# The down projection of a hybrid encoder block: kept activation sums, one more unit by seven products, weight loads in order

## The chip, the cores and the metric

The kernel runs on one core of a Trainium2 chip. The metric is the device time of one execution in microseconds. The median of three runs of the kernel before is 1112.83 us (1112.75 to 1113.62).

## The reference

One layer of an encoder block over 256 tokens of width 2048, in float32. After a mixing sub-layer (which the change doesn't touch) come a gated feed-forward part and a gated embedding:

```
hn   = rmsnorm(h, ffn_norm_pre)
up   = hn @ w_ffn_up                                  # 2048 -> 2 x 5632
gate, val = split(up, 2)
gate = dwconv_centred(gate, ffn_conv_w, ffn_conv_b)   # three taps along the tokens
ff   = (gelu(gate) * val) @ w_ffn_down                # 5632 -> 2048, "down"
h    = h + rmsnorm(ff, ffn_norm_post)
gate = sigmoid(rmsnorm(h, ple_norm_pre) @ w_ple_gate) # 2048 -> 2048
h    = h + rmsnorm(gate * (p @ w_ple), ple_norm_post)
```

## The kernel before

**Products.** Every float32 operand is split in two float32r parts, a high one (a cast, on ScalarE, L153) and a low one (the rest, a subtraction on VectorE, L154), by `split`. A product is then three matmuls: high by high, high by low, low by high. Matmuls have 128 x 128 stationary activations and 512 columns of weight.

**Down.** The hidden activations (44 blocks of 128 rows by 256 tokens, in six pages named `hid`) are multiplied by `w_down` in two column halves of 1024 (`sublayer`, which calls `token_major` once a half; names with `dn0` and `dn1`). Within a half the 44 blocks are taken in 22 units of two, u = 0 to 21. A plain unit loads one raw page of weight (128 x 2048, 1 MB), splits it in two pieces of 1024 columns and issues 24 matmuls. A unit named in `fast` (`dn_fast`, 17 units in the first half, 15 in the second) goes to `seven_products` instead: it treats the unit as a 2 x 2 block product and computes it with seven block products, 21 matmuls, at the price of sums. It needs sums of weight blocks (`add_blocks`, four additions of 128 x 512), and sums of activation blocks (`hid_sums`). After the last such unit `combine` adds the parts together. PSUM has six main banks and two others.

**Where the sums come from.** The weight sums are made ahead of time, during the gate/value matmuls of the feed-forward part: `block_sums` gives three jobs, fetch (a load on SP's queue), add (VectorE) and store (to DRAM, on POOL's queue). The list `which` names these units, and job i is placed at piece 45*i//10 + 4 of the 176 pieces of that stage, its add and store three pieces later; the last two stay in their pages. Down then loads the sums (tile names ending in `t`) beside the raw weight's last 1536 columns (names ending in `r`); the four splits of a unit are named `a` (512 columns of raw weight), `b` (1024 of raw weight), `d` and `c` (1024 each of the sums). The activation sums of thirteen pairs (`dn_stored`) are made in the same stage, stored to DRAM, and loaded back on POOL's queue into one of three `mid` tiles (L1096, names `hd`). The pairs of units 4, 9, 12 and 15 are not stored: `hid_sums` computes them in Down with four small VectorE operations (L826 to L829), a cast (L830) and a subtraction (L831), in each half anew. Each unit also splits its two activation blocks (`hid_split`, L968 and L969, two `hs` tiles).

**Output of a half.** After each half four 128 x 512 pieces are scaled and multiplied by the norm's gain into two pages `mg` (L877), one for each group of 128 tokens, both taken at the start of `sublayer`. After both halves the residual `h` (L887) is formed and transposed for the gate matmul.

**Order.** The framework schedules each engine's instructions by priority, dependence and free buffers; program order is the priority. `in_order` fixes the order by hand in the gate/value stage only. `load` issues a DMA on SP's queue; unless it is called with `ahead`, it is tied behind the last load that was noted in `last["dma"]`. The raw weight and sums loads are called with `ahead`, so the scheduler may swap them with each other. SP's queue works strictly in the order that results, and a load whose buffer isn't free holds those behind it. There are 13 pages of 128 x 2048 (hidden rows, sums, outputs), three raw tiles, five high and five low split tiles.

**The gate's first tile.** `at={11: first}` makes the second half of Down load the first tile of `w_gate` into a page (`gtf`) and split it into two more before unit 11, so that the gate matmul after Down can start at once. At the end of the second half (`NF // 2`) the residual is loaded back (`hb`) and the embedding's weight is split.

Of the kernel before, what the change touches and what calls it, by code (L numbers as in the profile page):

```python
# [17 lines left out]
P = 128  # L18
# [35 lines left out]
def build(nc, a, out):  # L54
# [6 lines left out]
    with tile.TileContext(nc) as tc, \  # L61
# [95 lines left out]
        def raw(name, src=None):  # L157
            r = wp.tile([P, 2048], F32, tag="raw", bufs=3, name=name)
            if src is not None:
                last["dma"] = load(r, src, True)  # L160
            return r

        class Panel:
# [28 lines left out]
                                                       op0=ALU.mult, op1=ALU.subtract)))  # L192

        LOW_LAST = (0, 2), (1,)
        work = []

        chain = {}
# [62 lines left out]
            nc.gpsimd.dma_start(t, r)  # L260
            sums_["wo", c * 1024, k] = t, False

        def add_blocks(r):

            v = r.rearrange("p (b c) -> p b c", b=4)
            for i, j in ((1, 0), (0, 3), (3, 1), (2, 3)):
                nc.vector.tensor_add(v[:, i], v[:, i], v[:, j])  # L267

        def seven_products(name, stage, w, k0, c0, a_, acc, alt, start, stop):

            if (stage, c0, k0) in sums_:
                r = raw(f"{name}r")
                last["dma"] = load(r[:, 512:], w[c0 // 1024, k0 // 2][:, 512:], True)
                t, held = sums_[stage, c0, k0]
                if not held:
                    t = page(f"{name}t")
                    last["dma"] = load(t, sums_[stage, c0, k0][0], True)
            else:  # L280
                r = t = raw(f"{name}r", w[c0 // 1024, k0 // 2])
            b11 = split(f"{name}a", r[:, 512:1024], 512)
            b2 = split(f"{name}b", r[:, 1024:], 1024)
            if r is t:
                add_blocks(r)
            t42 = split(f"{name}d", t[:, 1024:], 1024)
            t31 = split(f"{name}c", t[:, :1024], 1024)

            for x, (wh, wl), c, o, own in (
                    ("a11", b11, 0, alt[0], True), ("a12", b2, 0, acc[0][0], False), ("a22", t42, 0, acc[1][0], False),  # L290
                    ("s4", b2, 512, acc[0][1], False), ("s2", t42, 512, alt[3], True), ("s1", t31, 512, alt[1], True),
                    ("s3", t31, 0, alt[2], True)):
                xh, xl = a_[x]
                for q, (xx, ww) in enumerate(((xh, wh), (xh, wl), (xl, wh))):
                    mm(o, xx, ww[:, c:c + 512], own and start and q == 0, own and stop and q == 2)
# [561 lines left out]

        def sublayer(name, w, ks, get, gain, h, vnext, panel=Panel, fast=((), ()), sums=None, at=(), row=None, then=()):

            mg = [page(f"{name}m{t}") for t in range(2)]  # L860
            sq = [[], []]
            for half in range(2):

                alt = main(f"{name}s{half}") if fast[half] and half == 0 else []
                acc = [main(f"{name}a{half}{t}") for t in range(2)]
                if fast[half]:
                    alt += main(f"{name}s{half}") if half else []
                token_major(f"{name}{half}", w, half * 1024, ks, get, acc, 1, fast[half], alt, sums, at if half else ())
                for t in range(2):
                    for n in range(2):  # L870
                        q = tiny(f"{name}q{t}{half}{n}", 1)
                        junk = sp.tile([P, 512], F32, tag="junk", bufs=1, name=f"{name}j{t}{half}{n}")
                        c = slice(half * 1024 + n * 512, half * 1024 + (n + 1) * 512)
                        b = acc[t][n]
                        if row:
                            nc.scalar.activation(junk, b, AF.Square, scale=row[t], accum_out=q)
                            nc.vector.scalar_tensor_tensor(mg[t][:, c], b, row[t], gain[:, c], op0=ALU.mult, op1=ALU.mult)  # L877
                        else:
                            nc.scalar.activation(junk, b, AF.Square, accum_out=q)
                            nc.vector.tensor_mul(mg[t][:, c], b, gain[:, c])  # L880
                        sq[t].append(q)
            r = [rms(f"{name}{t}", sq[t], 1.0 / D) for t in range(2)]
            pan = panel(f"{name}x")
            for c in range(4):
                s = slice(c * 512, (c + 1) * 512)
                for t in range(2):
                    nc.vector.scalar_tensor_tensor(h[t][:, s], mg[t][:, s], r[t], h[t][:, s],  # L887
                                                   op0=ALU.mult, op1=ALU.add)
# [50 lines left out]
        for t in range(2):  # L939
            h_kept.append(dp.tile([P, D], F32, tag=f"h{t}", bufs=1, name=f"h_kept{t}"))  # L940
        pl_kept = dp.tile([P, D], F32, tag="pl", bufs=1, name="pl_kept")

        dn_fast, gt_fast = ((2, 3, 4, 5, 7, 8, 9, 10, 11, 12, 13, 14, 15, 16, 17, 18, 19), (2, 3, 4, 5, 7, 8, 9, 11, 12, 13, 14, 15, 16, 18, 19)), ((4, 5, 6), (1, 2, 3))

        dn_stored = (2, 3, 5, 7, 8, 10, 11, 13, 14, 16, 17, 18, 19)
        gt_ks = list(range(NK)), [0, 1, 8, 9, 10, 11, 12, 13, 2, 3, 4, 5, 6, 7, 14, 15]
        which = [("dn", w_down, c * 1024, 2 * u) for c in range(2) for u in dn_fast[c]] + \
            [("gt", w_gate, c * 1024, gt_ks[c][2 * u]) for c in range(2) for u in gt_fast[c]]
        jobs_at = [[] for _ in range(NPIECES)]

# [133 lines left out]
        def hid_get(k):  # L1084
# [47 lines left out]
        pl = [page("plb")]  # L1132
# [161 lines left out]
```

## Time and profile before

| what | value |
|---|---|
| median of three runs | 1112.83 us |
| the profiled execution | 1112.05 us |
| its span, first to last instruction | 1110.3 us |
| granted TensorE clock, mean | 0.997 |
| down, first half | 784.61 to 883.65 us |
| down, second half | 883.65 to 1006.12 us |

The page gives busy times by engine over the span; the windows give the same by stage, with the number of instructions in brackets, the granted clock, the busy share of the 16 DMA engines and what they moved. The chain of waits lists, in order of time, the work that ended last at each moment: start, length, engine, tile. A timeline row gives start and duration of one instruction and, in square brackets, how long its engine was idle before it and what ended that. PE is TensorE's matmul stream, PEld its weight loads, DVE VectorE, ACT ScalarE, POOL GpSimd, SPq the DMA queue of SyncE. A matmul of 512 columns is shown with about 0.39 us though the next starts 0.23 us later, so its row doesn't give its price; the distance of starts does.

### The profile page before, as it was taken

To read this page: it belongs to the slowest core of one execution; us is meant where nothing else is said; L and a number is where in the kernel's file an instruction comes from. 1 tells how busy PE (TensorE), PEld (TensorE's weight loads), DVE (VectorE), ACT (ScalarE), POOL (GpSimd) and SP (SyncE) were. 2 spreads that over 40 slices of the span, in tenths; PEclk is the share of its full clock that TensorE was granted. 3 is DMA by queue.
4 is the path that set the end of the run, shared out by engine and by line. 5 is a ranking of instruction groups with operands and counts; after the bars stand their busy time and mean duration, and the time that the engine had idled before them with its cause. 6 is when DMAs were issued, how large, how long until landed. Compare 5 with 4: busy or idle time off the path is not lost.

```text
span 1110.3 us, 16102 instructions
## 1 busy us (share of the span) xinstructions
PE 1101.8 (99%) x5958; PEld 950.0 (86%) x5958; DVE 968.6 (87%) x1351; ACT 727.8 (66%) x1061; POOL 78.1 (7%) x144
## 2 busy tenths in 40 slices
PE   9999999999999999999999999999999999999997
PEld 9999988888888888888888888888888888888875
DVE  6589997898868998888888888988899999999996
ACT  7958763555775565655655646657579877877682
POOL 0200000100100000000000000000000000021001
PEclk9999999999999999999999999999999999999998
DMA  9984356555589999999999998999999799995772
GB/s 364 367 332 185 115 197 259 208 218 201 182 344 399 397 416 349 384 365 361 391 362 379 359 390 342 405 355 424 362 390 401 299 341 408 412 391 225 276 294 76
DMA packets 56671, 358.83 MB, mean 323 GB/s; under 512 B 6288, under 2 KB 7184, under 8 KB 20880
## 3 DMA queue, kind: packets, MB, share of 16 engines
q1 hardware_dynamic: 45216, 296.87, 67.9%
q0 software_dynamic: 10944, 60.30, 14.4%
q8 instruction: 47, 0.77, 0.3%
q10 hardware_dynamic: 432, 0.62, 0.2%
q14 instruction: 32, 0.26, 0.1%
HBM read 304.82 MB, written 52.95 MB: 322 GB/s over the span
## 4 chain that ended last, share of the span: by engine, by line
PE 93%; ACT 3%; DMA 2%; DVE 1%; issue 1%; POOL 0%; SPq 0%; POOLq 0%; ACTq 0%
PE ga L90 22%; PE va L90 22%; PE dna L90 12%; PE woa L90 7%; PE xbc L90 5%; PE gt L90 5%; PE z L90 4%; PE dns L90 4%; PE dn0s L90 2%; PE dn1s L90 2%; DMA dtur<-w_dtu 2%; PE ple L90 1%; PE gts L90 1%; DMA x<-x 1%; PE yd L90 1%
## 5 line engine op out<-in xcount | busy, mean ns | idle before, releaser
L90 PE MATMUL ga<-wox,ug_0h 128*128 128x512 f32 x352 | 125.5, 395 | 0.0
L90 PE MATMUL ga<-wox,ug_1h 128*128 128x512 f32 x352 | 125.1, 394 | 0.0
L90 PE MATMUL va<-wox,uv_1h 128*128 128x512 f32 x352 | 124.8, 393 | 0.0
L90 PE MATMUL va<-wox,uv_0h 128*128 128x512 f32 x352 | 124.8, 393 | 0.0
L90 PE MATMUL ga<-wox,ug_1l 128*128 128x256 f32 x352 | 99.1, 282 | 0.0
L90 PE MATMUL va<-wox,uv_1l 128*128 128x256 f32 x352 | 99.1, 281 | 0.0
L90 PE MATMUL va<-wox,uv_0l 128*128 128x256 f32 x352 | 99.1, 281 | 0.0
L90 PE MATMUL ga<-wox,ug_0l 128*128 128x256 f32 x352 | 99.0, 281 | 0.0
L267 DVE TENSOR_TENSOR dnb<-dnb 128x512 f32<-128x512 f32 x128 | 88.3, 690 | 3.1
L90 PEld LDWEIGHTS va<-wox,uv_1h 128*128 128x128 f32 x352 | 66.1, 188 | 15.0
L90 PEld LDWEIGHTS va<-wox,uv_0h 128*128 128x128 f32 x352 | 66.1, 188 | 15.0
L90 PEld LDWEIGHTS ga<-wox,ug_1h 128*128 128x128 f32 x352 | 66.1, 188 | 15.0
L90 PEld LDWEIGHTS ga<-wox,ug_0h 128*128 128x128 f32 x352 | 66.1, 188 | 14.8
L90 PEld LDWEIGHTS ga<-wox,ug_0l 128*128 128x128 f32 x352 | 66.2, 188 | 0.1
L90 PEld LDWEIGHTS ga<-wox,ug_1l 128*128 128x128 f32 x352 | 66.2, 188 | 0.0
L90 PEld LDWEIGHTS va<-wox,uv_1l 128*128 128x128 f32 x352 | 66.2, 188 | 0.0
L90 PEld LDWEIGHTS va<-wox,uv_0l 128*128 128x128 f32 x352 | 66.2, 188 | 0.0
L245 POOL DMA_DIRECT2D dns<-dnb x30 | 16.1, 535 | 320.4 <-DVE dnb L267 291.6
L968 ACT CAST hs<-hid 128x512 fp32r<-128x512 f32 x44 | 27.1, 619 | 17.2 <-PE dna L90 17.1
L830 ACT CAST he<-he 128x512 fp32r<-128x512 f32 x13 | 8.1, 621 | 41.1 <-DVE he L829 41.1
L969 DVE TENSOR_TENSOR hs<-hid,hs 128x512 fp32r<-128x512 f32 x44 | 29.9, 685 | 3.4 <-ACT hs L968 3.4
L90 PE MATMUL dna<-dn_0h,hs 128*128 128x512 f32 x96 | 31.2, 393 | 0.0
(2334 smaller groups left out, 3249.6 us busy)
## 6 DMA issues: line engine op xcount, KB each, us to landing
dnb<-w_down SPq DMA_DIRECT2D x32, 1024.0 KB, 10.0
dns<-dnb POOLq DMA_DIRECT2D x30, 1024.0 KB, 5.8
hd<-hsum POOLq DMA_DIRECT2D x24, 512.0 KB, 8.4
zr<-w_z SPq DMA_DIRECT2D x8, 1024.0 KB, 4.8
dtur<-w_dtu SPq DMA_DIRECT2D x14, 528.0 KB, 8.7
dn1r<-w_down SPq DMA_DIRECT2D x7, 1024.0 KB, 9.3
hsum<-he POOLq DMA_DIRECT2D x13, 512.0 KB, 8.5
wo0r<-w_out_ SPq DMA_DIRECT2D x6, 1024.0 KB, 4.8
```

Source lines behind the costliest of these rows:

```text
L90: last["pe"] = ins(nc.tensor.matmul(o, lhsT, rhs, start=start, stop=stop, skip_group_check=True))
L245: nc.gpsimd.dma_start(t, pg[0])
L267: nc.vector.tensor_add(v[:, i], v[:, i], v[:, j])
L830: nc.scalar.copy(o[:, :512], s[:, :512])
L968: nc.scalar.copy(t[:, :512], hid_part(k))
L969: nc.vector.tensor_sub(t[:, 512:], hid_part(k), t[:, :512].bitcast(F32))
```

## The change

- The activation sums of units 4, 9, 12 and 15 are computed once, in the first half, into two pages (two pairs to a page), and used again in the second half.
- Unit 10 of the second half goes by seven products too (16 units instead of 15).
- In the second half, units 4 and 10 (`dn_here`) don't use stored weight sums: they load the whole raw page and add the blocks on the spot, on VectorE, into a fresh page. Unit 4's fetch, add and store leave the gate/value stage, and the list `which` has 37 entries instead of 38.
- The loads of the second half (`IN_ORDER`, names that begin with `dn1`) are each tied behind the load before.
- The gate's first tile is loaded before unit 15 (`first_raw`) and split before unit 17 (`first`).
- The pages of the weighed output hold one column half each instead of one token group each, and are taken at the end of their half.

```diff
         def raw(name, src=None):
             r = wp.tile([P, 2048], F32, tag="raw", bufs=3, name=name)
             if src is not None:
-                last["dma"] = load(r, src, True)
+                last["dma"] = load(r, src, not name.startswith(IN_ORDER))
             return r
...
+        IN_ORDER = ('dn1',)
...
+        APART = ("dn",)
+
-        def add_blocks(r):
+        def add_blocks(r, t=None):
 
             v = r.rearrange("p (b c) -> p b c", b=4)
-            for i, j in ((1, 0), (0, 3), (3, 1), (2, 3)):
-                nc.vector.tensor_add(v[:, i], v[:, i], v[:, j])
+            s = v if t is None else t.rearrange("p (b c) -> p b c", b=4)
+            for i, a, b in ((1, v, 0), (0, v, 3), (3, s, 1), (2, s, 3)):
+                nc.vector.tensor_add(s[:, i], v[:, i], a[:, b])
...
             if (stage, c0, k0) in sums_:
                 r = raw(f"{name}r")
-                last["dma"] = load(r[:, 512:], w[c0 // 1024, k0 // 2][:, 512:], True)
+                last["dma"] = load(r[:, 512:], w[c0 // 1024, k0 // 2][:, 512:], not name.startswith(IN_ORDER))
                 t, held = sums_[stage, c0, k0]
                 if not held:
                     t = page(f"{name}t")
-                    last["dma"] = load(t, sums_[stage, c0, k0][0], True)
+                    last["dma"] = load(t, sums_[stage, c0, k0][0], not name.startswith(IN_ORDER))
             else:
                 r = t = raw(f"{name}r", w[c0 // 1024, k0 // 2])
+                if stage in APART:
+                    t = page(f"{name}t")
+                    add_blocks(r, t)
...
-            mg = [page(f"{name}m{t}") for t in range(2)]
+            mg = []
...
                 token_major(f"{name}{half}", w, half * 1024, ks, get, acc, 1, fast[half], alt, sums, at if half else ())
+                mg.append(page(f"{name}m{half}"))
...
-        dn_fast, gt_fast = ((2, 3, 4, 5, 7, 8, 9, 10, 11, 12, 13, 14, 15, 16, 17, 18, 19), (2, 3, 4, 5, 7, 8, 9, 11, 12, 13, 14, 15, 16, 18, 19)), ((4, 5, 6), (1, 2, 3))
-
+        dn_fast, gt_fast = ((2, 3, 4, 5, 7, 8, 9, 10, 11, 12, 13, 14, 15, 16, 17, 18, 19), (2,3,4,5,7,8,9,10,11,12,13,14,15,16,18,19)), ((4, 5, 6), (1, 2, 3))
+
+        dn_here = (), (4,10,)
...
-        which = [("dn", w_down, c * 1024, 2 * u) for c in range(2) for u in dn_fast[c]] + \
+        which = [("dn", w_down, c * 1024, 2 * u) for c in range(2) for u in dn_fast[c] if u not in dn_here[c]] + \
...
+        own, own_pages = {}, []
+
         def hid_sums(k):
 
             (h1, l1), (h2, l2) = get_hid(k), get_hid(k + 1)
-            o = mid(f"hd{k}", F32R)
             if k in kept:
+                o = mid(f"hd{k}", F32R)
                 nc.gpsimd.dma_start(o.bitcast(F32), kept[k])
                 d = sums_in(o)
             else:
-                d = hid_sums_of(k, sp.tile([P, 512], F32, tag="junk", bufs=1, name=f"hs{k}"), o)
+                if k not in own:
+                    n = len(own)
+                    if n % 2 == 0:
+                        own_pages.append(page(f"hd{k}", F32R))
+                    own[k] = hid_sums_of(k, sp.tile([P, 512], F32, tag="junk", bufs=1, name=f"hs{k}"),
+                                         own_pages[-1][:, n % 2 * 1024:(n % 2 + 1) * 1024])
+                d = own[k]
...
+        def first_raw():
+
+            cur["gtf"] = page("gtf")
+            last["dma"] = load(cur["gtf"], w_gate[0, 0])
+
         def first():
 
-            r, hi, lo = page("gtf"), page("gtfh", F32R), page("gtfl", F32R)
-            last["dma"] = load(r, w_gate[0, 0])
+            r, hi, lo = cur.pop("gtf"), page("gtfh", F32R), page("gtfl", F32R)
...
-                      fast=dn_fast, sums=hid_sums, at={11: first, NF // 2: lambda: (ple_parts(), back())}, row=rf, then={1: lambda: second(0), 2: lambda: second(1)})
+                      fast=dn_fast, sums=hid_sums, at={15: first_raw, 17: first, NF // 2: lambda: (ple_parts(), back())}, row=rf, then={1: lambda: second(0), 2: lambda: second(1)})
```

More of the change, by code (lines that the diff above doesn't have):

```diff
@@ L871, in sublayer @@
                         q = tiny(f"{name}q{t}{half}{n}", 1)
+                        m = mg[half][:, t * 1024 + n * 512:t * 1024 + (n + 1) * 512]
                         junk = sp.tile([P, 512], F32, tag="junk", bufs=1, name=f"{name}j{t}{half}{n}")
@@ L876, in sublayer @@
                             nc.scalar.activation(junk, b, AF.Square, scale=row[t], accum_out=q)
-                            nc.vector.scalar_tensor_tensor(mg[t][:, c], b, row[t], gain[:, c], op0=ALU.mult, op1=ALU.mult)
+                            nc.vector.scalar_tensor_tensor(m, b, row[t], gain[:, c], op0=ALU.mult, op1=ALU.mult)
                         else:
                             nc.scalar.activation(junk, b, AF.Square, accum_out=q)
-                            nc.vector.tensor_mul(mg[t][:, c], b, gain[:, c])
+                            nc.vector.tensor_mul(m, b, gain[:, c])
                         sq[t].append(q)
@@ L886, in sublayer @@
                 for t in range(2):
-                    nc.vector.scalar_tensor_tensor(h[t][:, s], mg[t][:, s], r[t], h[t][:, s],
+                    m = mg[c // 2][:, t * 1024 + c % 2 * 512:t * 1024 + (c % 2 + 1) * 512]
+                    nc.vector.scalar_tensor_tensor(h[t][:, s], m, r[t], h[t][:, s],
                                                    op0=ALU.mult, op1=ALU.add)
```

## The prediction

> **What bounds the kernel now.** I read the page first, then the busy time by stage, then the chain of waits in order of time through the down projection, where the change lies, and last the rows of each engine there.
>
> ```profile
> span 1110.3 us, 16102 instructions
> PE 1101.8 (99%) x5958; PEld 950.0 (86%) x5958; DVE 968.6 (87%) x1351; ACT 727.8 (66%) x1061; POOL 78.1 (7%) x144
> ...
> L267 DVE TENSOR_TENSOR dnb<-dnb 128x512 f32<-128x512 f32 x128 | 88.3, 690 | 3.1
> ```
>
> TensorE is busy for 99% of the span. A page that says so can still hide a stage with another limit, so the next view is by stage: the last of gate/value (762 to 785), down's first half, its second half, the inside of that, and the rest.
>
> ```profile
> core 0: us, PE busy (x) PEld busy (x) DVE busy (x) ACT busy (x) POOL busy (x), PEclk, DMA share, GB/s
> 762.28:784.61 22.33, 22.33 (x130) 19.61 (x129) 21.12 (x28) 14.06 (x23) 1.21 (x3) 1.00 1.01 421
> 784.61:883.65 99.04, 99.04 (x430) 80.43 (x430) 93.07 (x112) 82.32 (x101) 5.92 (x11) 1.00 0.93 363
> 883.65:1006.12 122.47, 122.47 (x532) 99.65 (x532) 116.87 (x144) 91.40 (x120) 14.10 (x16) 1.00 0.95 376
> ...
> 899.86:995.07 95.21, 95.21 (x414) 77.48 (x413) 90.29 (x111) 76.66 (x95) 11.91 (x11) 1.00 0.99 397
> ```
>
> In each of these stretches TensorE never rests, at clock 1.00. But in the last one VectorE is busy 90.29 of 95.21 us and the DMA engines 0.99 of the time: three resources are close to full together. TensorE ends the stage, with VectorE and the loads right behind.
>
> The chain of waits gives the price of a unit (two k blocks of the weight):
>
> ```profile
> 945.25 5.55 PE dna L90 x24
> 950.80 0.69 PE dns L90 x3
> ...
> 955.65 0.69 PE dns L90 x3
> ```
>
> Unit 10 is now a plain unit: 24 products in 5.55 us (0.231 each). Unit 11 is of seven products: 21 matmuls from 950.80 to 955.65, 4.85 us. No gap lies between them.
>
> **The change part by part.**
>
> Unit 10 by seven products: three matmuls fewer, 3 x 0.231 = **0.69 us off TensorE**. This is on the path. Everything else must only not stand in its way.
>
> VectorE first. A unit of seven products, here unit 12, costs it:
>
> ```profile
> 953.14 0.68 DVE L969 TENSOR_TENSOR hs<-hid,hs 128x512 fp32r<-128x512 f32 x1
> 953.74 0.68 DVE L154 TENSOR_TENSOR dn124al<-dn124r,dn124ah 128x512 fp32r<-128x512 f32 x1
> 954.34 1.22 DVE L154 TENSOR_TENSOR dn124bl<-dn124r,dn124bh 128x1024 fp32r<-128x1024 f32 x1
> 955.48 1.22 DVE L154 TENSOR_TENSOR dn124dl<-dn124t,dn124dh 128x1024 fp32r<-128x1024 f32 x1
> 956.61 1.22 DVE L154 TENSOR_TENSOR dn124cl<-dn124t,dn124ch 128x1024 fp32r<-128x1024 f32 x1
> 957.75 0.69 DVE L969 TENSOR_TENSOR hs<-hid,hs 128x512 fp32r<-128x512 f32 x1
> ```
>
> From start to start it is 4.61 us a unit, against TensorE's 4.85: 0.60 for each 512 columns, 1.13 for 1024. A plain unit costs 0.60 + 2 x 1.13 = 2.87.
>
> The Trainium skill, page "VectorE: DVE Perf Modes", section "The DRAIN you can't avoid", says that the next operation does not start until the pipe is empty. By it a unit would cost the sum of the durations, 2 x 0.68 + 3 x 1.22 = 5.02 us, more than 4.85, and VectorE would set the pace (the first rival). The trace differs: dn124al ran from 953.74 to 954.42 and dn124bl started at 954.34. The same page's section "Two Vector instructions with no wait between them" has the next one start earlier, and with that the rows agree.
>
> Added to VectorE in the second half: four adds on the spot in units 4 and 10. The trace has adds of this shape only in place (L267, 690 ns); written to another page their cost lies between 0.60 (the pitch above) and 0.69. I take 0.60, since they stand in a row without waits: 2.40 a unit, 4.80 in all. Unit 10 also turns from 2.87 to 4.61: 1.74. Together +6.54.
>
> Removed: the sums of four pairs (units 4, 9, 12, 15), made in the first half and now kept. One in the second half is:
>
> ```profile
> 949.93 0.29 DVE L826 TENSOR_TENSOR hs<-hid 128x128 f32<-128x128 f32 x1
> 950.14 0.28 DVE L827 TENSOR_TENSOR hs<-hid 128x128 f32<-128x128 f32 x1
> ...
> L831 DVE TENSOR_TENSOR hd<-hs,hd 128x512 fp32r<-128x512 f32 x4 | 2.7, 685 | 0.7 <-ACT hd L830 0.7
> ```
>
> Four small ones 0.21 apart and one of 0.60: 1.44 a pair, 5.76 for four. ScalarE loses four casts with them and gains unit 10's; at 76.66 busy of 95.21 it has room. Net on VectorE: +0.8 us over the half, whose 116.87 of 122.47 leave 5.6.
>
> What matters is when. The two halves of the gate's first tile are split on VectorE too, 2 x 1.13 = 2.27, now ahead of unit 11's work; these move to unit 17, a plain unit. So before unit 11, VectorE loses 2.27 and about two and a half pairs' sums (3.6), and gains 6.54: +0.7 against 50 us of work. The closest place is unit 4:
>
> ```profile
> 914.85 1.22 DVE L154 TENSOR_TENSOR dn18dl<-dn18t,dn18dh 128x1024 fp32r<-128x1024 f32 x1
> ...
> 916.93 0.40 PE L90 MATMUL dna<-dn18dl,hs 128*128 128x512 f32 x1
> ...
> 906.28 0.69 DVE L831 TENSOR_TENSOR hd<-hs,hd 128x512 fp32r<-128x512 f32 x1 [0.69 <-ACT hd L830]
> ```
>
> The low part of unit 4's sums ends at 916.07 and is used at 916.93: 0.86 us to spare. The adds put 2.40 ahead of it. Taken away ahead of it are unit 4's own sums (0.82 + 0.60), the wait of 0.69 that they brought at 906.28, and 0.41 of unit 9's: 2.52. So the spare stays near 0.9. On ScalarE the cast of the sums now waits for these adds instead of for a transfer; behind it stand the next units' casts, and VectorE's subtractions wait for those in turn.
>
> For unit 17: VectorE had rests in units 18 and 19 already.
>
> ```profile
> 986.07 0.69 DVE L969 TENSOR_TENSOR hs<-hid,hs 128x512 fp32r<-128x512 f32 x1 [1.12 <-ACT hs L968]
> ...
> 992.51 1.23 DVE L154 TENSOR_TENSOR dn_0l<-dn1r,dn_0h 128x1024 fp32r<-128x1024 f32 x1 [0.87 <-ACT dn_0h L153]
> ```
>
> These two rests, 2.0 us, and the 1.5 us less that it has had to do up to unit 16 (6.54 - 2.27 - 5.76) take the tile's 2.27. Cost zero; with that cover gone it would be at most 2.27.
>
> Transfers. Bytes and times to landing:
>
> ```profile
> hd<-hsum POOLq DMA_DIRECT2D x11, 512.0 KB, 8.3
> gtf<-w_gate SPq DMA_DIRECT2D x1, 1024.0 KB, 12.0
> dn122t<-dns SPq DMA_DIRECT2D x1, 1024.0 KB, 9.1
> dn122r<-w_down SPq DMA_DIRECT2D x1, 768.0 KB, 8.1
> ```
>
> Unit 4 loads 1024 KB of raw weight where it loaded 768 + 1024: -768. Unit 10 adds one load of kept sums: +512. The gate tile's 1024 leave the stretch before unit 11 and come back ahead of unit 15. So 1280 KB less up to unit 11 (3.3 us at 397 GB/s), 256 KB less in all. In the gate/value stage one fetch, four adds and one store go, and the later jobs move four or five pieces forward; TensorE waits for none of them there (22.33 of 22.33), so I count nothing, gain or loss.
>
> The loads in order:
>
> ```profile
> 934.15 0.33 SPq L120 DMA_DIRECT2D dn122r<-w_down  x1
> 938.76 0.33 SPq L120 DMA_DIRECT2D dn124r<-w_down  x1
> 939.13 0.43 SPq L120 DMA_DIRECT2D dn122t<-dns  x1
> ...
> 948.31 1.05 ACT L153 CAST dn122dh<-dn122t 128x1024 fp32r<-128x1024 f32 x1 [0.93 <-DMA dn122t<-dns]
> ```
>
> Today unit 12's raw load stands ahead of unit 11's sums, waits 4.6 us for its buffer, and ScalarE later waits 0.93 for the sums. In order, this swap goes. In return a sums load that waits for a page now holds every later weight load on SP's queue, and behind those the casts. The trace has no such wait by itself; the nearest row on either side is this one, 0.93 gained or lost on ScalarE, and TensorE did not feel it. I take zero.
>
> The pages: two for the kept sums come, the two of the weighed output are taken one per half instead of both at the start. In the first half the count is the same, in the second one more is held until unit 15. The output's writes keep their shape; the first half's four now ask for a page when they come, and a late page would hold VectorE's queue behind them and the PSUM banks that the second half needs. Of 13 pages six hold the hidden rows and two the kept sums, so five are left for loads and this. I take nothing; at most one wait as above.
>
> The sum: -0.69 us, nothing else on the path. The profiled execution took 1112.05 (its span 1110.3 and 1.75 around it): 1111.36. The runs' median is 0.78 above it, so **1112.1**.
>
> **The rivals.**
>
> *VectorE sets the pace, and TensorE's 0.69 turns into waits.* For it: 90.29 of 95.21 us busy, and no rest from 944 to 980. Against it: 4.61 against 4.85 a unit and net only +0.8. Time: 1112.8.
>
> *Slower: the adds come late at units 4 and 10.* If the freed 2.52 us lie where VectorE could not use them (unit 4's raw page not there in time, or the adds put ahead of unit 3's subtractions), TensorE waits 2.40 - 0.86 = 1.54 at unit 4. At unit 10 VectorE has 2.40 + 1.74 more and TensorE 0.69 less; the tile's 2.27 and a spare of 0.86 as at unit 4 are taken off: 1.70. With -0.69 that is +2.55: 1115.4. It decides as soon as the adds start later than about 0.9 us after where the old sums stood. Against it: the raw page of unit 4 was asked for at 899.40, and the adds are wanted after 906.
>
> *The tile's load ahead of unit 15 makes the last units' loads late.* 1024 KB are 2.6 us at 397 GB/s. Today the last such unit has little to spare:
>
> ```profile
> 989.29 1.22 DVE L154 TENSOR_TENSOR dn138dl<-dn138t,dn138dh 128x1024 fp32r<-128x1024 f32 x1
> ...
> 991.66 0.39 PE L90 MATMUL dna<-dn138dl,hs 128*128 128x512 f32 x1
> ```
>
> 990.51 to 991.66 is 1.15, so 1.5 of waiting: 1113.6. Against it: 3.3 us of transfers went before.
>
> *Faster: waits in the gate stage go as well.* Its weight loads wait in eight places, the longest of them
>
> ```profile
> PEld gt L90 <- ACT pl L900: 0.6, 1, 0.6
> ```
>
> and all together some 2.4 us. Nothing in the change aims at them, but the loads' order shifts there too. Half of them gone: 1110.9.
>
> **How the numbers follow.** Forecast 0.56, VectorE's pace 0.14, late adds 0.16, late loads 0.08, gate waits 0.06. The range runs from the gate case to just under the late adds' full price: 1111.0 to 1115.2; beyond lie half of the late adds' case and half of the gate case, some 0.11. A measurement of this kernel can tell about 0.2% from no change, 2.2 us: under 1110.6 is faster, over 1115.1 slower. Faster 0.03 (half the gate case), slower 0.15 (most of the late adds), same 0.82.
>
> **What would show it.** Right: second half 121.8 us with TensorE without a rest, unit 10 in 4.85, one DMA wait less at unit 11, VectorE still below TensorE in 899 to 995. Wrong: a wait of TensorE's weight loads for a subtraction of units 3, 4, 10 or 11 (late adds), or of units 15 to 19 with ScalarE waiting for a DMA before them (late loads); SP's queue waiting long for a page with weight loads behind it. A stretch before 784 or after 1006 that differs by over 1 us would mean that the scheduling moved where I counted nothing.

## The result, and the profile after

The changed kernel takes 1114.32 us (median of 22 runs, 1113.49 to 1115.58). The kernel before takes 1112.58 beside it (22 runs, 1112.02 to 1113.97). The ratio is 1.0014, with a 95% interval of 1.0008 to 1.0020: slower by about 1.7 us. That is inside what I had called no change (0.2%) and inside the range, but the interval leaves one out, and the forecast had 0.7 us faster. The profiled execution took 1113.99.

The page of the changed kernel looks almost like the one before:

```profile
span 1112.2 us, 16069 instructions
PE 1102.3 (99%) x5955; PEld 949.6 (85%) x5955; DVE 967.0 (87%) x1337; ACT 727.3 (65%) x1059; POOL 73.7 (7%) x144
...
L271 DVE TENSOR_TENSOR dnb<-dnb 128x512 f32<-128x512 f32 x124 | 85.6, 690 | 3.1
```

TensorE has its three matmuls less (5955 for 5958) and VectorE four adds less in the gate/value stage (124 for 128). The windows of the changed kernel say in which stage the time went:

```profile
785.22:884.13 98.91, 98.91 (x430) 80.50 (x430) 91.45 (x107) 81.17 (x99) 5.91 (x11) 1.00 0.95 370
884.13:1008.07 123.94, 122.81 (x530) 98.29 (x529) 116.93 (x134) 90.99 (x118) 10.85 (x17) 1.00 0.93 368
```

Down's first half is as long as before (98.91 for 99.04), and so is what follows Down (1008.07 to 1112.2, 104.13 for 104.18). Down starts 0.6 us later. That comes from the first stages, where the change does nothing (the sixteen matmuls `mx` near the start begin at 64.24 for 63.65); in the traces of the kernels below, whose first stages are the same, Down starts anywhere from 784.3 to 785.9. The second half takes 123.94 us. Before it took 122.47, and the forecast was 121.78. So 2.16 us of waits stand against the 0.69 saved. (One thing to mend: the cut at 883.65, which I called the start of the second half, is where TensorE begins the first half's last two plain units; the second half itself starts 11.1 us later. Both kernels are cut at the same work, so the differences hold.)

The waits of TensorE's weight loads in that stage, the largest first (engine, line, what was waited for, us in total, times, the longest):

```profile
PEld dna L90 <- ACT hs L979: 1.4, 1, 1.4
PEld dna L90 <- ACT dn132dh L153: 0.6, 1, 0.6
PEld dna L90 <- DVE dn132bl L154: 0.4, 1, 0.4
PEld dns L90 <- DVE dn132cl L154: 0.4, 1, 0.4
...
PEld dna L90 <- DVE dn120dl L154: 0.2, 1, 0.2
...
PEld dna L90 <- DVE dn18dl L154: 0.2, 1, 0.2
```

Before there was not one. The names place them: `dn132` is unit 16, and the `hs` is the activation split of unit 17. The units that add on the spot, 4 (`dn18`) and 10 (`dn120`), have 0.2 us here, and their matmuls show no gap: by the starts of the matmuls TensorE loses 0.90 us at unit 16 and 1.26 at unit 17, together the 2.16, and nothing before them. The chain of waits of the changed kernel shows what ended last there:

```profile
960.42 15.21 DMA dn132t<-dns
...
975.73 1.06 ACT dn132dh L153
976.78 0.04 issue
976.83 0.97 PE dna L90 x3
...
980.89 0.02 ACTq L153
980.91 0.61 ACT hs L979
981.52 0.04 issue
981.56 5.82 PE dna L90 x24
```

The sums of unit 16 took 15.21 us from issue to landing. The cast `dn132dh` starts as soon as they are there, and ScalarE reaches the activations of unit 17 only at 980.91, with TensorE already waiting. VectorE's timeline in the same place:

```profile
972.95 1.22 DVE L154 TENSOR_TENSOR gtfl<-gtf,gtfh 128x1024 fp32r<-128x1024 f32 x1
974.09 0.68 DVE L154 TENSOR_TENSOR dn132al<-dn132r,dn132ah 128x512 fp32r<-128x512 f32 x1
974.69 1.22 DVE L154 TENSOR_TENSOR dn132bl<-dn132r,dn132bh 128x1024 fp32r<-128x1024 f32 x1
975.83 1.22 DVE L154 TENSOR_TENSOR gtfl<-gtf,gtfh 128x1024 fp32r<-128x1024 f32 x1
976.96 1.22 DVE L154 TENSOR_TENSOR dn132dl<-dn132t,dn132dh 128x1024 fp32r<-128x1024 f32 x1
```

Both halves of the gate tile's split (`gtfl`) stand ahead of `dn132dl`. The program has them ahead of unit 17, but the scheduler put them between the pieces of unit 16. Two suspects therefore meet here: transfers that land late, and the split's place.

For the transfers, compare how long the same loads took from issue to landing. First the kernel before, then the changed one:

```profile
dn130t<-dns SPq DMA_DIRECT2D x1, 1024.0 KB, 10.5
dn132t<-dns SPq DMA_DIRECT2D x1, 1024.0 KB, 10.7
```

```profile
hd<-hsum POOLq DMA_DIRECT2D x12, 512.0 KB, 8.4
...
gtf<-w_gate SPq DMA_DIRECT2D x1, 1024.0 KB, 13.5
dn130t<-dns SPq DMA_DIRECT2D x1, 1024.0 KB, 13.6
dn132t<-dns SPq DMA_DIRECT2D x1, 1024.0 KB, 15.2
```

And the windows over units 2 to 6, 7 to 12 and 13 to 16 of the second half, again before and after:

```profile
907.50:931.00 23.50, 23.50 (x103) 19.13 (x102) 23.33 (x32) 18.49 (x23) 1.61 (x3) 1.00 0.97 377
931.00:960.00 29.00, 29.00 (x127) 23.60 (x126) 27.65 (x34) 25.13 (x32) 1.61 (x3) 1.00 1.01 414
960.00:981.60 21.60, 21.60 (x96) 17.57 (x95) 21.60 (x25) 18.04 (x23) 6.83 (x4) 1.00 0.99 400
```

```profile
907.50:931.00 23.50, 23.50 (x103) 18.96 (x102) 23.29 (x27) 17.81 (x21) 1.61 (x3) 1.00 0.85 321
931.00:960.00 29.00, 29.00 (x127) 23.52 (x126) 27.97 (x33) 25.24 (x31) 2.15 (x4) 1.00 1.01 399
960.00:981.60 21.60, 20.47 (x87) 15.21 (x85) 20.18 (x22) 16.66 (x21) 4.36 (x4) 1.00 1.02 420
```

The last two columns are the DMA engines' share and GB/s. From 931 to 981.6 both kernels moved the same 20.6 MB (29.0 us at 414 and 21.6 at 400; 29.0 at 399 and 21.6 at 420) with the engines full. Before that stretch the changed kernel left room: 321 for 377 GB/s over 23.5 us are 1.3 MB that were not moved. That is about what the change takes away early. What it brings late is unit 10's 512 KB, and the place of the tile's 1024. The kernel before asked for the tile at 927.36 and had it 12.0 us later, so part of it moved in the full stretch there too; the changed kernel asks for it at 951.68, in the middle of that stretch and right ahead of unit 15's loads.

### The profile page after: what moved, and what is told of

Its sections match the earlier page's. It is cut to its first block, busy times and chain, and to the rows that moved or that the text cites. A ratio compares the mean times of both kernels' runs of the same rounds, so it can differ in the third digit from the quotient of the medians.

```text
span 1112.2 us, 16069 instructions
## 1 busy us (share of the span) xinstructions
PE 1102.3 (99%) x5955; PEld 949.6 (85%) x5955; DVE 967.0 (87%) x1337; ACT 727.3 (65%) x1059; POOL 73.7 (7%) x144
## 4 chain that ended last, share of the span: by engine, by line
PE 93%; DVE 3%; ACT 2%; DMA 1%; issue 1%; POOL 0%; POOLq 0%; SPq 0%; ACTq 0%
PE ga L90 22%; PE va L90 22%; PE dna L90 10%; PE woa L90 7%; PE xbc L90 5%; PE gt L90 5%; PE dtu L90 4%; PE z L90 4%; PE dns L90 3%; PE dn0s L90 2%; DMA dn132t<-dns 1%; PE ple L90 1%; PE dn1s L90 1%; PE gts L90 1%; PE yd L90 1%
## 5 line engine op out<-in xcount | busy, mean ns | idle before, releaser
L271 DVE TENSOR_TENSOR dnb<-dnb 128x512 f32<-128x512 f32 x124 | 85.6, 690 | 3.1
```

Source lines behind the costliest of these rows:

```text
L271: nc.vector.tensor_add(s[:, i], v[:, i], a[:, b])
```

## The experiments

Three mechanisms were in question. **Transfers** (theory L in the expectations): the loads of units 10 to 16 ask for more than the DMA engines move, and the loads of units 15 and 16 land late. **Place** (S): the tile's split, 2.27 us of VectorE, stands ahead of unit 16's sums and unit 17. **Adds** (V): VectorE's adds on the spot, the late-adds rival of the prediction. Each kernel ran up to 11 times beside the kernel before. A time is the median, with its ratio to the kernel before and the 95% interval. Each edit is to the changed kernel unless it says otherwise. A median also holds what the other stages do: in the profiled execution of the first kernel below, the slowest of its eleven (1113.64), the gate stage takes 105.19 us for 104.18, with a wait of 1.5 for `gt112dh`, which nothing in the edit touches. So where medians lie less than about 1 us apart, the length of the second half in the trace, cut at the same work, says more.

**Which part of the change costs.** Unit 10 plain again, all else as changed:

```diff
-... (2,3,4,5,7,8,9,10,11,12,13,14,15,16,18,19) ...
+... (2,3,4,5,7,8,9,11,12,13,14,15,16,18,19) ...
-        dn_here = (), (4,10,)
+        dn_here = (), (4,)
```

> The changed kernel, with unit 10 of the second half plain again (24 products, no adds). Theories S and L: the waits at units 16 and 17 stay and TensorE has 0.69 us more: 1114.5 to 1115.0, ratio 1.0018 to 1.002. Theory V: VectorE has 4.1 us less to do, the waits go: 1112.5 to 1113, ratio about 1.000.

Measured: 1112.38, 0.9999 (0.9990 to 1.0008). Its second half, as one window:

```profile
884.13:1006.61 122.48, 122.48 (x532) 99.59 (x532) 113.11 (x129) 89.73 (x116) 9.21 (x16) 1.00 0.93 369
```

TensorE doesn't rest. So everything else, the tile at 15 and 17 among it, comes out even with the kernel before. Unit 10 by seven products, meant to give 0.69, costs 1.9. The time is about what theory V expected, but a plain unit 10 does without its 512 KB of kept sums as well as without its adds, so this run doesn't tell the two apart.

The kernel before with nothing but unit 10 by seven products and its adds on the spot:

```diff
-        dn_fast, ... (2, 3, 4, 5, 7, 8, 9, 11, 12, 13, 14, 15, 16, 18, 19)
+        dn_fast, ... (2, 3, 4, 5, 7, 8, 9, 10, 11, 12, 13, 14, 15, 16, 18, 19)
...
+                if stage == "dn":
+                    t = page(f"{name}t")
+                    add_blocks(r, t)
```

> The kernel before with one part alone: unit 10 by seven products, its blocks added on the spot; the tile stays at unit 11, no sums are kept, the loads are not in order. The prediction's 0.69 us come only if VectorE's 4.1 us more beside unit 10 are hidden. It has the tile's 2.27 us right behind them: I expect 1.5 to 3 us of waits at units 10 to 12 and 1113.5 to 1115, ratio 1.001 to 1.002; if VectorE's spare there is larger than the rows show, 1112.0, ratio 0.9994.

Measured: 1115.46, 1.0027 (1.0016 to 1.0037). Here the gate tile still stands ahead of unit 11, so the waits come right there, and ScalarE's largest wait is for a transfer:

```profile
PEld dna L90 <- ACT dn122dh L153: 1.2, 1, 1.2
PEld dns L90 <- DVE dn122al L154: 1.1, 1, 1.1
...
ACT dn122dh L153 <- DMA dn122t<-dns: 2.4, 1, 2.4
```

The kernel before with nothing but the tile's load at 15 and its split at 17 (`first_raw` and `first` as in the change):

```diff
-... at={11: first, NF // 2: lambda: (ple_parts(), back())} ...
+... at={15: first_raw, 17: first, NF // 2: lambda: (ple_parts(), back())} ...
```

> The kernel before with one part of the change alone: the gate tile loaded before unit 15 and split before unit 17. The order of the tile's load and split among the other instructions is that of the changed kernel. If the tile's place alone costs what the change lost (L and S without help), TensorE waits 1.5 to 2.2 us at units 16 and 17: 1114 to 1114.7, ratio 1.0014 to 1.002. If it only costs together with unit 10 by seven products (whose adds hold its raw tile longer and so move all later loads back), there is no wait and the time is that of before, ratio 0.9995 to 1.0005.

Measured: 1113.71, 1.0010 (1.0001 to 1.0019), second half 123.56. Its waits:

```profile
PEld dna L90 <- DVE dn132dl L154: 0.6, 1, 0.6
PEld dna L90 <- DVE hs L969: 0.5, 1, 0.5
PEld dns L90 <- DVE dn132cl L154: 0.4, 1, 0.4
```

All are for VectorE at units 16 and 17, and ScalarE waits for no transfer there, although `dn132t` now takes 13.2 us to land (10.7 before). Without the kept sums, the split's place alone costs about 1.1 us.

The loads of the second half not in order:

```diff
-        IN_ORDER = ('dn1',)
+        IN_ORDER = ('none',)
```

> The changed kernel without the order of loads (the second half's loads may be swapped again by the scheduler). All of theories S, L and V leave the waits at 16 and 17 as they are: 1114.0 to 1114.7, ratio 1.0012 to 1.002. If the order is a cause (a sums load that waits for its page or raw tile holds the later ones), the waits shrink and the time is 1112.5 to 1113.3. If the order is a help, as the prediction had it, it is slower than the changed kernel by up to 0.5 us.

Measured: 1115.47, 1.0027 (1.0018 to 1.0036). ScalarE then waits 2.5 us for unit 15's raw load. The order is worth 1.1 to 1.4 us to the changed kernel (by the medians and by the ratios, whose intervals touch).

**Adds or transfers.** Two kernels with unit 10 plain as above do one of its burdens for nothing: a load of 512 KB of sums that nobody reads, or four adds into a page that nobody reads.

```diff
+        def idle_load():
+            o = mid("idle", F32R)
+            nc.gpsimd.dma_start(o.bitcast(F32), kept[20])
...
+... at={10: idle_load, 15: first_raw, 17: first, ...
```

> The changed kernel with unit 10 plain (no waits, 1112.4) and at unit 10 a load of 512 KB of activation sums that nothing reads. If unit 10's own bytes are what makes the later loads late, the sums of unit 16 land 1.3 us later, ScalarE waits for them and TensorE for 0.5 to 1.3 us: 1113 to 1113.7, ratio 1.0005 to 1.001. If VectorE's adds are the cause, no change: 1112.2 to 1112.6, ratio 0.9998 to 1.0001.

```diff
+                if name == "dn1" and u == 10:
+                    add_blocks(r, page("idle"))
```

> The changed kernel with unit 10 plain and four adds of its raw blocks into a page that nothing reads: VectorE's 2.4 us alone, with no more bytes and no seven products. If they hold the raw tile and so the later loads, the gate tile's load is asked for 2 to 3 us later than with unit 10 plain (948.5) and the waits at 16 and 17 come back in part: 1113 to 1114, ratio 1.0005 to 1.0013. If bytes are the cause: 1112.2 to 1112.6.

Measured: 1112.78, 1.0000 (0.9992 to 1.0009) with the load, and 1112.45, 0.9998 (0.9989 to 1.0007) with the adds. The adds bring no wait of TensorE. The load makes `dn132t` land 1.4 us later (beside the plain kernel, both counted from the start of the half), which is about what 512 KB take at 400 GB/s, and TensorE's weight loads wait 0.6 at unit 17. The load comes through POOL's queue and delays loads of SP's. The Trainium skill, in "DMA: Bandwidth & Descriptors", section "Issuing engines are not separate DMA queues", says that whichever engine issues, the transfers run on the same 16 DMA engines; the 1.4 us agree with it. With unit 10 plain, either burden alone costs too little to see in the time.

The opposite: unit 10 by seven products with its weight sums stored ahead, as the other units have them. VectorE has 2.40 us less to do, and the transfers 768 KB more.

```diff
-        dn_here = (), (4,10,)
+        dn_here = (), (4,)
```

> The changed kernel with unit 10's weight sums made ahead and stored, as for the other units, instead of added on the spot; VectorE has 2.4 us less to do in unit 10, and 768 KB more come in. If the adds cost (they hold the raw tiles of units 10 to 12 longer, so that the loads of units 13 to 16 and the gate tile are asked for some 3 us later), the tile's load is asked for at about 948.5 as with unit 10 plain, and the waits at 16 and 17 shrink to about those of the tile's split: 1112.6 to 1113.4, ratio 1.000 to 1.0008. If the bytes cost, the sums of unit 16 land later still: 1114.5 to 1115.5, ratio 1.0018 to 1.0026.

Measured: 1114.85, 1.0022 (1.0013 to 1.0031). No better, and ScalarE's waits for transfers are longer:

```profile
ACT dn130dh L153 <- DMA dn130t<-dns: 1.4, 1, 1.4
ACT dn_0h L153 <- DMA dn1r<-w_down: 0.8, 1, 0.8
ACT dn132dh L153 <- DMA dn132t<-dns: 0.8, 1, 0.8
```

With the adds gone the loss stays, so it doesn't need them. That they do no harm isn't shown by this run, since 768 KB more come in. They do hold raw tiles longer: the gate tile is asked for at 951.68 in the changed kernel, at 949.4 here and at 948.5 with unit 10 plain.

**The tile's place.** Eight kernels move the load or the split. "Tied" holds the split's two pieces behind the work that stands ahead of them on ScalarE and VectorE, so that the scheduler can't pull them forward:

```diff
-                ready[f"gt00_{j}"] = split(f"gt00_{j}", r[:, c], 1024)
+                with tc.issue_after(last["act"]), tc.issue_after(last["dve"]):
+                    ready[f"gt00_{j}"] = split(f"gt00_{j}", r[:, c], 1024)
```

Tied only, load and split still at 15 and 17:

> The changed kernel, with the two halves of the gate tile's split tied behind the split of unit 16 on ScalarE and VectorE; its load stays ahead of unit 15. Theory S (the tile's split stands ahead of unit 16's sums and of unit 17 on both engines): TensorE's waits at units 16 and 17, about 2.2 us, shrink to under 0.5, and the time is 1112.0 to 1112.6, a ratio to before of 0.999 to 1.000. Theory L (the tile's load makes the sums of unit 16 land late): ScalarE still waits for dn132t and the time stays at 1113.8 to 1114.4, ratio 1.001 to 1.0015. Theory V (the adds of units 4 and 10 hold VectorE up): as L, with the waits at units 4, 5, 10 and 11.

Measured: 1114.55, 1.0018 (1.0009 to 1.0027). With the split out of the way of unit 16, ScalarE still waits for its transfers (1.6 for `dn132t`, 1.0 for `dn132r`), and unit 17's wait grows to 2.1.

Load before 11, split at 17 as in the change:

```diff
-... at={15: first_raw, 17: first, NF // 2: lambda: (ple_parts(), back())} ...
+... at={11: first_raw, 17: first, NF // 2: lambda: (ple_parts(), back())} ...
```

> The changed kernel, with the gate tile loaded before unit 11 as in the kernel before, its split at unit 17 as in the change: the split's place among the other instructions is the same as in the changed kernel. Theory S: the waits at 16 and 17 stay, 1113.8 to 1114.5, ratio about 1.0014. Theory L: dn132t lands in time, 1112.0 to 1112.6, ratio under 1.000. Both at work: 1113.

Measured: 1113.04, 1.0005 (0.9996 to 1.0013). ScalarE's waits for `dn130t` and `dn132t` are gone, and 1.3 us come back, 1.43 by the second half (122.51 us for 123.94). Waits of 0.4 each stay for `hs`, `dn132dl` and `dn132cl`; TensorE loses 0.8 us there (`hs` comes behind a wait of ScalarE's, 1.1 for unit 17's raw weight). `dn132dl` stands right behind the second piece of the tile's split on VectorE (976.38 after 975.24).

Both before 11, as the kernel before has them (`at={11: lambda: (first_raw(), first()), ...`):

> The changed kernel, with the gate tile loaded and split before unit 11 as in the kernel before. Theories S and L: no waits at units 15 to 17, and VectorE has 2.27 us more to do ahead of unit 11; with what the prediction counted as spare it holds, 1112.0 to 1112.8, ratio 0.9995 to 1.000. Theory V: VectorE, already pressed by the adds of unit 10, comes 1 to 2 us late at units 11 and 12: 1113 to 1114, ratio 1.0005 to 1.001.

Measured: 1113.15, 1.0004 (0.9995 to 1.0013). The wait moves to unit 11: 1.1 for `dn122al`.

Load before 11, split tied at 20; and load before 18, split tied at 20:

> The changed kernel with the gate tile loaded before unit 11 and its split tied behind unit 19's: neither the load nor the split stands in the stretch of units 11 to 16. If late loads (L) and the split's place (S) are all that the change lost, TensorE has no wait there: the second half takes 121.8 to 122.1 us against 123.9 in the changed kernel, and the time is 1111.9 to 1112.3, ratio 0.9993 to 0.9998. If VectorE's adds in units 4 and 10 are a cause of their own (V), waits stay at units 4, 10 and 11 and the second half takes over 122.4: ratio 1.000 or more.

> The changed kernel with the gate tile loaded before unit 18, behind unit 17's plain load, and split behind unit 19's. Theory L: units 11 to 16 have their loads in time, and the tile's 2.6 us of transfer falls where the next four units ask for less; no waits, second half 121.8 to 122.1, ratio 0.9993 to 0.9998. Against it: the loads of units 18 and 19 come 2.6 us later, ScalarE waits for dn136t, and 0.5 to 1 us is lost there: ratio about 1.000.

Measured: 1113.80, 1.0008 (0.9999 to 1.0017), and 1117.64, 1.0043 (1.0030 to 1.0056). In both, the sums of the half's parts at its end (`dna`, `combine`) come late behind the split, by 1.3 and 1.9 us. In the first, ScalarE also waits for transfers although the tile is loaded early (1.5 for `dn132t`, 1.6 for unit 17's raw weight); I have no cause for that. The load before 18 makes unit 18's raw weight 2.1 us late.

Load before 6, split at 7; the same with unit 10's weight sums stored; and load before 6, split tied at 18:

> The changed kernel with the gate tile loaded before unit 6 and split before unit 7, beside the plain unit 6: in the changed kernel SP's queue asks for nothing from 902.5 to 910, and the DMA engines are at 0.87 from 900 to 931. If the tile's place (load and split) is what turns unit 10's gain into a loss, neither stands in a full stretch now: TensorE's waits come to under 0.5 us, second half 121.8 to 122.2, 1111.9 to 1112.3, ratio 0.9993 to 0.9998, faster than both kernels. If VectorE's load at units 10 and 11 costs by itself, waits of 0.5 to 1 us stay there: ratio about 1.000.

> Both of the two before: unit 10's weight sums stored, the tile loaded before unit 6 and split before unit 7. If VectorE sets the end in units 10 to 16, this is the fastest, 1111.8 to 1112.1, ratio 0.9992 to 0.9996. If the transfers do, the 768 KB more make unit 14 to 18 wait for their loads: ratio about 1.000.

> The changed kernel with the gate tile loaded before unit 6, where the transfers have room, and its split tied behind unit 17's, so that only one page is held meanwhile and ScalarE and VectorE have no work of the tile before unit 18. If place of load and split are all that is wrong with the change, no waits: second half 121.8 to 122.2, 1111.9 to 1112.4, ratio 0.9993 to 0.9999. If the loads of units 13 to 16 are late without the tile too, waits of 0.5 to 1.5 us stay: ratio 1.0003 to 1.001.

Measured: 1114.07, 1.0014 (1.0005 to 1.0023); 1112.99, 1.0002 (0.9993 to 1.0011); 1114.40, 1.0016 (1.0008 to 1.0025). With the split at 7, TensorE waits at unit 10 for ScalarE's casts (1.0 for `dn120dh`, 0.8 for `dn120bh`); with no adds on the spot in unit 10 these waits are gone, and 1.1 us by the medians, though the intervals overlap. So with the split close by, the adds can cost. With the split tied at 18 the loads of units 15 and 16 are in time, and TensorE waits at units 18 to 20 for ScalarE and VectorE (1.2 for `dn_0l`, 0.7 for `dn138dh`). So wherever the split is put, it meets late loads or full engines, and both transfers and place were still suspects.

**Fewer bytes in the full stretch.** Unit 10's activation sums kept in a page too, as a fifth pair (512 KB less, nothing more for VectorE in the second half):

```diff
-        dn_stored = (2, 3, 5, 7, 8, 10, 11, 13, 14, 16, 17, 18, 19)
+        dn_stored = (2, 3, 5, 7, 8, 11, 13, 14, 16, 17, 18, 19)
```

> The changed kernel with the activation sums of unit 10 too kept in a page from the first half (a third page) instead of stored and loaded: 512 KB less in the second half, VectorE there unchanged. If unit 10's bytes are the cause: the waits at 16 and 17 shrink to those of the split's place, 1112.8 to 1113.4, ratio 1.0003 to 1.0008. If VectorE's adds are: 1114.0 to 1114.5, ratio 1.0013 to 1.0017.

Measured: 1113.00, 1.0004 (0.9995 to 1.0013). This gives back 1.3 us, as the early load of the tile did, but only 0.84 by the second half (123.10 us). What is left: 0.8 for `hs`, behind ScalarE's wait of 1.7 for unit 17's raw weight, and 0.6 for `dn132dl` and 0.4 for `dn132cl`, which look like the split's place. Two kernels with both reliefs were to tell whether it is. They add to this edit the tile's load before 11, or before 6, with the split at 17 as the change has it:

> Unit 10 keeps its activation sums (512 KB less) and the gate tile's 1024 KB are issued before unit 11; the split stays at unit 17. Full transfers in units 11 to 16: each relief alone gave 1113.0; if they add, ScalarE waits for no transfer before the subtractions of units 15 to 17, and only the split's place is left, 0.4 to 0.7 us of TensorE's waits: 1112.2 to 1112.7, ratio 0.9996 to 1.0001. Split's place alone (rival): it decides what is left after either relief, so both together stay at 1113.0.

> As the run before, with the tile's load ahead of unit 6, where the transfers have room before the stretch fills. Full transfers: 1111.9 to 1112.6, at or just under the kernel before, waits of TensorE only behind the split at units 16 and 17, 0.4 to 0.7 us. Split's place alone (rival): 1113.0. If the tile's pages held early make the loads of units 10 to 13 late, waits at units 10 to 12 take the place: 1113 to 1114.

Measured: 1112.29, 0.9997 (0.9989 to 1.0006), and **1111.04, 0.9986 (0.9977 to 0.9995)**. By the medians the two reliefs together give back 2.0 and 3.3 us.

The first of the two takes 122.50 us in its second half, as long as with the early load alone (122.51). So by the trace the fifth kept pair adds nothing to the early load; the medians are 0.75 apart, and their intervals overlap. ScalarE waits for none of the transfers of units 15 and 16 any more, and TensorE still loses 0.8 us at units 16 and 17. Its weight loads wait there for VectorE alone (0.5 for `hs`, 0.4 each for `dn132dl` and `dn132cl`), on which `dn132dl` follows right behind the second piece of the tile's split:

```profile
974.84 1.22 DVE L154 TENSOR_TENSOR gtfl<-gtf,gtfh 128x1024 fp32r<-128x1024 f32 x1
975.98 1.22 DVE L154 TENSOR_TENSOR dn132dl<-dn132t,dn132dh 128x1024 fp32r<-128x1024 f32 x1
...
977.26 0.50 PE L90 MATMUL dna<-dn132dl,hs 128*128 128x512 f32 x1
```

The time is what full transfers expected, the length of the half what the rival expected; in both, what is left is the split's place.

The second kernel comes out below its expected 1111.9 to 1112.6 and beats the kernel before, by 0.6 to 2.6 us. Its second half in one window, and its transfers in three:

```profile
883.87:1005.62 121.75, 121.75 (x529) 98.90 (x529) 116.82 (x134) 91.45 (x118) 23.57 (x17) 1.00 0.94 371
```

```profile
907.50:931.00 23.50, 23.50 (x104) 18.96 (x102) 23.02 (x26) 17.67 (x22) 1.61 (x3) 1.00 0.95 364
931.00:960.00 29.00, 29.00 (x127) 23.64 (x126) 28.21 (x33) 25.32 (x32) 1.62 (x3) 1.00 1.00 404
960.00:981.60 21.60, 21.60 (x95) 17.55 (x94) 21.60 (x24) 19.41 (x23) 12.13 (x3) 1.00 1.03 419
```

```profile
gtf<-w_gate SPq DMA_DIRECT2D x1, 1024.0 KB, 7.6
...
dn130t<-dns SPq DMA_DIRECT2D x1, 1024.0 KB, 9.8
dn132t<-dns SPq DMA_DIRECT2D x1, 1024.0 KB, 9.9
```

The tile now moves in the room of units 2 and 3 (364 GB/s up to 931 for 321) and lands in 7.6 us. The stretch behind it is as full by the share as ever, yet unit 16's sums land 9.9 us after their issue for 15.2. TensorE doesn't rest: 121.75 us with 529 matmul records, against 122.48 with 532 in the kernel with unit 10 plain. The difference, 0.73, is the saving that was forecast. VectorE in the same place:

```profile
973.50 1.25 DVE L154 TENSOR_TENSOR gtfl<-gtf,gtfh 128x1024 fp32r<-128x1024 f32 x1
974.64 1.25 DVE L154 TENSOR_TENSOR dn132dl<-dn132t,dn132dh 128x1024 fp32r<-128x1024 f32 x1
975.77 1.25 DVE L154 TENSOR_TENSOR dn132cl<-dn132t,dn132ch 128x1024 fp32r<-128x1024 f32 x1
976.91 1.26 DVE L154 TENSOR_TENSOR gtfl<-gtf,gtfh 128x1024 fp32r<-128x1024 f32 x1
```

The split is still here, a full 2.27 us, but its second piece now stands behind unit 16's sums, where the scheduler put it by itself. `dn132dl` ends at 975.89, where the changed kernel had 978.18: 2.0 us earlier, counted from the start of the half. Ahead of the sums the piece would have made `dn132dl` 1.13 later, and that had 0.73 to spare, so at least 0.4 of the 0.75 us between the second halves of these two kernels is the piece's place. Since ScalarE waited for no transfer of units 15 and 16 in the first of them either, it may be all. No run has the load before 6 with both pieces left ahead of unit 16's sums, so what the still earlier load gives beyond another order on VectorE isn't shown.

Not all of the 1.7 us of the medians is placed: 0.72 lie in the second half and 0.5 in the gate stage (1005.62 to 1109.3 is 103.68 for 104.18, where the wait for `pl` is gone), and the profiled execution of the kernel before was 0.66 under its median here.

## Why the prediction was wrong

**The saving, 0.69: right.** It appears in full where nothing stands in its way (0.73 between two kernels without rests).

**Transfers: the step that failed.** The prediction wrote "1280 KB less up to unit 11 (3.3 us at 397 GB/s), 256 KB less in all", and held it against the late-loads rival: "3.3 us of transfers went before". That treats bytes saved early as a credit for later. They were none: SP's queue waits for raw tiles to come free (from 902.5 to 910.0, for unit 3's `dn16bl`), so the engines simply moved 321 GB/s for 377 before 931 and didn't work ahead. From 931 on they were full in both kernels, and there the change adds unit 10's 512 KB and asks for the tile's 1024 behind unit 14's loads, right ahead of unit 15's. The sum should have been made over that stretch alone: +512 KB, and the tile asked for in the middle of it instead of at its start. Loading the tile before 11 and nothing else gives back 1.43 of the 2.16 us. The late-loads rival had the right mechanism (the tile's load makes loads behind it late), and the sign that the prediction had set for it came: waits at units 16 and 17 with ScalarE waiting for a DMA before them. It worked its price out from unit 19, which was not late, so that 1.5 us comes near the 1.43 is luck; its chance, 0.08, was far too small.

**The split's place: also wrong, and second.** "Cost zero", I said, because VectorE rests 2.0 us in units 18 and 19. The scheduler put the split ahead of unit 16's sums, not there. And those rests were no room: the rows that I quoted name ScalarE as what ended them, and when the split was tied at 18, TensorE waited for ScalarE and VectorE. In the kernel before, with only the tile's load and split moved, it costs 1.1 us; in the changed kernel with the tile loaded before 11, and unit 15's and 16's transfers in time, about 0.8, with the fifth pair kept or not. Of the kernels with the split at 17 and unit 10 by seven products, it costs nothing only in the one where the scheduler put its second piece behind unit 16's sums. The 2.16 us are thus about 1.4 for the late transfers and 0.7 for the place.

**VectorE: right in the sum, too hopeful in the detail.** Its busy time in the half grew from 116.87 to 116.93, less than the 0.8 that I had. But the spare at unit 4 did not stay near 0.9: `dn18dl` ended 0.15 us before its use, and unit 10's `dn120dl` 0.14. A weight load of TensorE waited 0.2 at each and no matmul was late, so the late-adds rival did not come true, and four adds beside a plain unit 10 cost nothing. The spare stays at 0.3 in units 11 and 12, where it was 0.84 before, but by unit 14 it is back at 0.79 (0.96 before). That the adds have a part in the loss at units 16 and 17, other than by the later loads, is not shown.

**Loads in order: taken as zero, worth about 1.1 us in the changed kernel.** The swap at unit 11 and its wait went, as said: ScalarE no longer waits for `dn122t`.

**Pages and the gate/value stage: right**, nothing to be seen in either. The pages for a fifth kept pair cost TensorE nothing visible either.

## What to carry to other kernels

Sum the bytes over the stretch in which the transfers are full, not over the stage: bytes taken away ahead of it gave nothing here, and a load that is asked for in the middle of it makes the loads behind it late. An engine's rest is room only if what ended it is not itself the bottleneck behind it: read the releaser in the bracket before putting work there. And when two reliefs give the same and don't add up, look at what ends the waits that are left. Here each came to 1113.0 by the median; with the early load in, TensorE's waits at unit 16 were for VectorE behind the split, and they went only when a piece of the split stood elsewhere.

## What the runs showed of the hardware

Here the DMA share and the GB/s don't tell how late a load is. In the window from 960 to 981.6 the changed kernel and the best one read 1.02 and 420, 1.03 and 419, while the same 1024 KB took 15.2 and 9.9 us to land; the gate tile's 1024 KB, asked for at 907.4, took 7.6. The time to landing is the number that showed the backlog. An add of 128 x 512 into another page, which the trace of before did not have, took 0.60 us from start to start (912.79 to 913.39), as the prediction took it; in place, four in a row take 2.86 in the trace of before.
